# A sliding-window copy on one core: one row of the last plain unit leaves outside its scatter, in sixteen pieces

## The chip, the core and the metric

The kernel runs on one core of a Trainium2 chip. A core has several engines that work side by side, each with an instruction stream of its own: TensorE (PE, idle here), VectorE (DVE), ScalarE (ACT), GpSimd (POOL) and SyncE (SP). They work on SBUF, an on-chip memory of 128 partitions. Sixteen DMA engines move data between SBUF and device memory. A DMA is issued by SyncE, ScalarE or GpSimd, and is cut into packets that the DMA engines work off; when a DMA engine has done its share, it writes a 4-byte completion packet.

The metric is the time of one execution on the device in microseconds (us), as the median of several runs.

## The reference

The input x is a float32 tensor of 16 images with 64 channels of 64 x 64. Every 8 x 8 window at a stride of 4 is copied out, 15 x 15 windows for each image, with all channels. Nothing is computed; the kernel is data movement, 16.8 MB in and 62.9 MB out, since each input value lands in up to four windows.

```python
def reference(x, window_size, stride):          # 8 and 4
    n_h = n_w = 15
    result = np.zeros((batch, n_h, n_w, c, window_size, window_size), dtype=np.float32)
    for i in range(n_h):
        for j in range(n_w):
            h_start = i * stride
            w_start = j * stride
            result[:, i, j] = x[:, :, h_start:h_start + window_size, w_start:w_start + window_size].copy()
    return result
```

One output row, for an image and a window (i, j), is 64 channels x 8 x 8 floats: 4,096 floats, 16 KB in one piece of device memory.

## The kernel before

**Layout.** The input lies in the tile L. A partition is 64 * ch + 4 * b + q: ch is the half of the channels (2), b the image (16), q the quarter of the image's 64 rows (4). So partitions 0 to 63 hold the lower half of the channels and 64 to 127 the upper one. Of each quarter's 16 rows, a window may start at 4 slots, s = 0 to 3.

**Loads.** Part of the input comes first into the tiles of the output buffer GG, by DMAs of SyncE and ScalarE (L115), and is copied from there to L (L132). The rest is loaded straight into L by SyncE and GpSimd (L58).

**Units of work.** GG has four buffers of 16 KB for each partition; `tile_()` hands them out in turn. A unit fills one buffer so that each partition holds one finished output row, and then sends it out. Filling is copying with a column offset, by ScalarE (L164, L178, L203), by VectorE (copies, and stream shuffles at L167 and L174).

- `part(y, j)` (six times, L144 with idx_y0 or idx_y1) does the early work, on the half of the images that has been loaded first.
- `unit(j, 0)` is a plain unit: for window column j it fills slot 0 for partitions 0 to 63 and slot 1 for 64 to 127, and scatters with the index tile idx. It is done eight times, for j from 6 to 13.
- `unit(j, 2)` is a crossing unit for the slots 2 and 3, whose last windows reach into the next quarter. It scatters with idx_hi or idx_lo in turn, eight times with idx_lo and seven with idx_hi. In these a partition with q = 3 has no slot 3, and its row is skipped: its index is set beyond the bound that the scatter tests. In idx_lo these are the partitions 3, 7, ... 63, in idx_hi 67, 71, ... 127.
- At the end, window column 14 is done for slots 0 and 1 in two buffers (L251) and leaves by two plain stores of SyncE (L253), 64 rows of 16 KB each.

**Scatter.** `scatter` (L143) is one indirect DMA on GpSimd's queue: partition p's 16 KB go to the output row that the index tile names for p, plus a constant offset for j and s. An index of at least 16 * 225 is dropped. The stores are declared independent of each other (`free`), since each writes rows of its own.

**Order.** The program order is the order of the loops at L227 to L238: three parts; three pairs of a part and a plain unit; then five rounds of three crossing units and one plain unit. In the last round the plain unit (j = 13) has its copies split in another way between ScalarE and VectorE (the argument list with `ACT_C`), because the last plain unit is the last scatter; the two stores of SyncE come after it. The index tiles are computed once, at the start, by some twenty small integer operations of VectorE on 128 x 1 tiles (L72 to L101).

Of the kernel before, what the change touches and what calls it, by code (L numbers as in the profile page):

```python
# [10 lines left out]
def kernel(  # L11
# [7 lines left out]
    nc = tc.nc  # L19
# [10 lines left out]
    ALU = mybir.AluOpType  # L30
    CH = 2
    HQ = P // (B * CH)
    CL = C // CH
    RB = H // HQ
    NSLOT = RB // ST
# [26 lines left out]
    def itile(name):  # L62
        return ipool.tile([P, 1], i32, name=name)

    pi, tb, tq, tc_, th, idx, idx_y0, idx_y1, idx_lo, idx_hi = (
        itile(n) for n in ("pi", "tb", "tq", "tc", "th", "idx", "idx_y0", "idx_y1", "idx_lo", "idx_hi")
    )
    FAR = float(2 * B * NWIN)
    nc.gpsimd.iota(pi[:, :], pattern=[[0, 1]], base=0, channel_multiplier=1)  # L69

    def bits(d, shift, mask):
# [2 lines left out]
    def mul(d, a, m):  # L74
        nc.vector.tensor_scalar(out=d[:, :], in0=a[:, :], scalar1=float(m), scalar2=None, op0=ALU.mult)  # L75

    def tt(d, a, b, op):
        nc.vector.tensor_tensor(out=d[:, :], in0=a[:, :], in1=b[:, :], op=op)  # L78
# [14 lines left out]

    nc.vector.tensor_scalar(out=tq[:, :], in0=tq[:, :], scalar1=float(HQ - 1), scalar2=FAR, op0=ALU.is_equal, op1=ALU.mult)
    tt(th, tc_, tq, ALU.mult)
# [3 lines left out]
    tt(idx_lo, tb, th, ALU.add)  # L99
    mul(th, tc_, NW)  # L100
    tt(idx_lo, idx_lo, th, ALU.add)  # L101


    NG = 4
# [7 lines left out]
    for q in range(HQ):  # L112
        for ch in range(CH):
            s = S[ch][QP + q : QP + q + (B - 1) * HQ + 1 : HQ]
# [24 lines left out]
    def free(st):  # L139
        tc.declare_no_dep(st.ins, group="stores", reason="each store writes rows of its own")  # L140
        tc.add_to_no_dep_group("stores", st.ins)

    def scatter(g, ix, j, s):  # L143
        st = nc.gpsimd.indirect_dma_start(  # L144
            out=o_v,
            out_offset=bass.IndirectOffsetOnAxis(ap=ix[:, 0:1], axis=0),
            in_=g.rearrange("p c r w -> p (c r w)"),
            in_offset=None,
            element_offset=(s * NW + j) * CFREE,
            bounds_check=B * NWIN - 1,  # L150
            oob_is_err=False,
        )
        free(st)

    def fill(g, half, s, j, lo, n, copies):

        d = slice(half * HP + lo, half * HP + lo + n)
        cols = slice(j * ST, j * ST + WS)
        for ch in (half, 1 - half):
            f = slice(ch * HP + lo, ch * HP + lo + n)  # L160
            cs = slice(ch * CL, (ch + 1) * CL)
            copy = copies[ch != half]
            if s < NSLOT - 1:
                copy(out=g[d, cs, :, :], in_=L[f, :, s * ST : s * ST + WS, cols])  # L164
            else:
                copy(out=g[d, cs, 0:ST, :], in_=L[f, :, s * ST : RB, cols])
                nc.vector.stream_shuffle(out=g[d, cs, ST:WS, :], in_=L[f, :, 0:ST, cols], mask=nxt)  # L167

    act, dve = nc.scalar.copy, nc.vector.tensor_copy
# [6 lines left out]
    def split(k, other):  # L176
        def both(out, in_):
            act(out=out[:, 0:k], in_=in_[:, 0:k])  # L178
            other(out=out[:, k:], in_=in_[:, k:])  # L179

        return both

    mix = split(CL // 4, shf)
# [3 lines left out]
    ACT_C = 12  # L187
    at = 0

    def tile_():  # L190
        nonlocal at
        at += 1
        return G[(at - 1) % NG]
# [15 lines left out]

    crossed = 0  # L210

    def unit(j, s, copies=(shf, mix)):
        nonlocal crossed
        g = tile_()
        if s == 0:
            fill(g, 0, 0, j, 0, HP, (act, copies[0]))
            fill(g, 1, 1, j, 0, HP, (act, copies[1]))
            scatter(g, idx, j, s)
        else:

            turn = 1 - crossed % 2
            crossed += 1
            fill(g, turn, s, j, 0, HP, (act, act))
            fill(g, 1 - turn, s + 1, j, 0, HP, (shf, mix))
            scatter(g, (idx_hi, idx_lo)[turn], j, s)
# [3 lines left out]
    plain = [(j, 0) for j in range(2 * EARLY, NW - 1)]  # L229
    cross = [(j, 2) for j in range(NW)]  # L230
    for n in range(EARLY):
        part(1, 2 * n)
        unit(*plain.pop(0), (dve, dve))
    while plain:
        for w in cross[:3]:
            unit(*w)
        cross = cross[3:]
        unit(*plain.pop(0), *([] if len(plain) else [(split(ACT_C, shf), split(ACT_C, dve))]))  # L238


    o_e = out.rearrange("b i j c r w -> j b i (c r w)")
    j = NW - 1
    for s in range(2):
        g = tile_()
# [44 lines left out]
```

## Time and profile before

| what | value |
|---|---|
| median of 3 runs | 186.99 us (186.84 to 187.19) |
| profiled execution, time | 187.06 us |
| profiled execution, span from first to last instruction | 185.3 us |
| VectorE busy | 154.2 us, 83% |
| ScalarE busy | 150.7 us, 81% |
| GpSimd busy | 48.3 us, 26% |
| DMA packets | 10,980, 75.81 MB, mean 409 GB/s |
| GpSimd's DMA queue (q0) | 8,656 packets, 65.55 MB, 84.8% of the 16 engines' span |
| SyncE's DMA queue (q1) | 1,744 packets, 8.13 MB, 11.0% |
| ScalarE's DMA queue (q10) | 576 packets, 2.10 MB, 3.1% |
| instruction queue (q14) | 4 packets, 0.03 MB |

In a line on a group or on the timeline, "L144 POOL DMA_INDIRECT out_dram<-GG,idx" is the instruction at line 144, on GpSimd, that writes the output from GG with the index tile idx. "SPq" and "POOLq" are the instruction queues of SyncE and GpSimd; a time there is the time of issuing. A line with 40 digits cuts the span (or the window asked for) into 40 slices, and each digit is the busy share in tenths. In an answer on the DMA queues over a window, packets are counted by their start, and "under 512 B" counts the completion packets and other small ones. The trace also holds every DMA packet with its start, its time, its size and its queue, but not the number of its DMA engine; where a text speaks of packet records, it means these.

### The profile page before, as it was taken

How to read it: one execution, taken by the hardware profiler on the slowest of the kernel's cores; microseconds unless marked ns; L12 is line 12 of the kernel's file. 1: busy time of each engine (PE TensorE's matmuls, PEld its weight loads, DVE VectorE, ACT ScalarE, POOL GpSimd, SP SyncE). 2: the span in 40 equal slices, each digit the busy share in tenths (PEclk: the TensorE clock that was granted, in tenths of full speed). 3: DMA queues.
4: the chain of work that ended last, by engine and by line, in shares of the span. 5: the costliest groups of instructions: out<-in, count | busy, mean ns of one | idle time of the engine just before them, and what ended most of it. 6: DMA issues, size and time to landing. Idle time of an engine off the chain costs nothing.

```text
span 185.3 us, 597 instructions
## 1 busy us (share of the span) xinstructions
DVE 154.2 (83%) x213; ACT 150.7 (81%) x100; POOL 48.3 (26%) x50
## 2 busy tenths in 40 slices
DVE  5002998999999999799999999999999999999600
ACT  0002999999999999998899999998999999899600
POOL 7400652033308071422222222222222222222000
DMA  4999999999999999999999999999999999999995
GB/s 151 398 410 399 402 402 399 390 382 426 433 424 435 428 428 439 432 430 424 435 430 432 428 432 428 439 417 435 424 423 428 410 435 414 421 428 403 442 414 216
DMA packets 10980, 75.81 MB, mean 409 GB/s; under 512 B 3280, under 2 KB 3280, under 8 KB 7376
## 3 DMA queue, kind: packets, MB, share of 16 engines
q0 software_dynamic: 8656, 65.55, 84.8%
q1 hardware_dynamic: 1744, 8.13, 11.0%
q10 hardware_dynamic: 576, 2.10, 3.1%
q14 instruction: 4, 0.03, 0.0%
HBM read 16.78 MB, written 62.91 MB: 430 GB/s over the span
## 4 chain that ended last, share of the span: by engine, by line
ACT 28%; DVE 28%; DMA 27%; issue 8%; POOL 2%; ACTq 1%; DVEq 0%; PEldq 0%
DVE GG L174 17%; ACT GG L203 17%; DMA L<-in_x_dram 14%; DMA out_dram<-GG,idx 13%; DVE GG L167 11%; ACT GG L164 7%; ACT GG L251 3%; POOL L L58 2%; ACT GG L178 1%; ACTq L284 0%; ACTq L203 0%; POOL pi L69 0%; DVEq L174 0%; PEldq L284 0%; ACTq L164 0%
## 5 line engine op out<-in xcount | busy, mean ns | idle before, releaser
L164 ACT COPY GG<-L 64x2048 f32<-64x2048 f32 x46 | 87.3, 1897 | 5.1 <-DMA out_dram<-GG,idx 2.7
L174 DVE STREAM_SHUFFLE GG<-L 64x1024 f32<-64x1024 f32 (+4 forms) x39 | 53.0, 1359 | 1.3
L167 DVE STREAM_SHUFFLE GG<-L 64x1024 f32<-64x1024 f32 x30 | 38.4, 1281 | 0.0
L203 DVE COPY GG<-L 32x2048 f32<-32x2048 f32 x30 | 36.6, 1219 | 1.8 <-DMA L<-in_x_dram 0.8
L203 ACT COPY GG<-L 32x2048 f32<-32x2048 f32 x18 | 34.1, 1897 | 0.7 <-DMA L<-in_x_dram 0.3
L132 DVE COPY L<-GG 32x2048 f32<-32x2048 f32 x10 | 11.9, 1234 | 13.7 <-DMA GG<-in_x_dram 13.6
L144 POOL DMA_INDIRECT out_dram<-GG,idx_y x6 | 11.0, 1838 | 26.3 <-DVE GG L203 13.2
L58 POOL DMA_DIRECT2D L<-in_x_dram x16 | 12.8, 809 | 19.0 <-DMA L<-in_x_dram 18.5
L144 POOL DMA_INDIRECT out_dram<-GG,idx_lo x8 | 7.7, 961 | 30.8 <-DVE GG L167 23.2
L132 ACT ACT_TABLE_LOAD x1 | 1.3, 1283 | 17.2 <-DMA GG<-in_x_dram 17.2
L144 POOL DMA_INDIRECT out_dram<-GG,idx x8 | 9.7, 1217 | 17.4 <-DVE GG L174 6.8
L144 POOL DMA_INDIRECT out_dram<-GG,idx_hi x7 | 6.7, 961 | 26.6 <-DVE GG L167 22.9
L132 ACT COPY L<-GG 32x2048 f32<-32x2048 f32 x6 | 11.2, 1894 | 0.1
L178 ACT COPY GG<-L 64x256 f32<-64x256 f32 (+2 forms) x21 | 10.2, 484 | 0.5
L164 DVE COPY GG<-L 64x2048 f32<-64x2048 f32 x6 | 7.3, 1222 | 0.2
L251 DVE COPY GG<-L 32x1280 f32<-32x1280 f32 x8 | 6.5, 818 | 0.4 <-DMA out_dram<-GG,idx_hi 0.3
L251 ACT COPY GG<-L 32x768 f32<-32x768 f32 x8 | 6.6, 829 | 0.1
L174 DVE LOAD_MASK_SELECT GG<-L x39 | 0.4, 9 | 1.4 <-ACT GG L164 1.0
L72 DVE TENSOR_SCALAR tb<-pi 128x1 int32<-128x1 int32 x1 | 0.2, 154 | 1.0 <-POOL pi L69 1.0
L179 DVE COPY GG<-L 64x1280 f32<-64x1280 f32 x1 | 0.9, 877 | 0.0
L78 DVE TENSOR_TENSOR th<-tc,tq 128x1 int32<-128x1 int32 x2 | 0.3, 156 | 0.0
L75 DVE TENSOR_SCALAR th<-tc 128x1 int32<-128x1 int32 x2 | 0.3, 154 | 0.0
(21 smaller groups left out, 3.0 us busy)
## 6 DMA issues: line engine op xcount, KB each, us to landing
L<-in_x_dram POOLq DMA_DIRECT2D x10, 768.0 KB, 18.4
L<-in_x_dram SPq DMA_DIRECT2D x6, 640.0 KB
GG<-in_x_dram ACTq DMA_DIRECT2D x4, 512.0 KB, 14.4
GG<-in_x_dram SPq DMA_DIRECT2D x4, 512.0 KB, 14.8
out_dram<-GG SPq DMA_DIRECT2D x2, 1024.0 KB, 10.1
L<-in_x_dram POOLq DMA_DIRECT2D x6, 128.0 KB, 18.2
out_dram<-GG,idx POOLq DMA_INDIRECT x8, 12.4
out_dram<-GG,idx_lo POOLq DMA_INDIRECT x8, 10.3
```

The costliest lines, as they stand in the source:

```text
L58: eng.dma_start(out=L[p0 : p0 + QP - HQ + 1 : HQ, c0:c1, :, :], in_=x_v[ch, y, q, :, c0:c1, :])
L75: nc.vector.tensor_scalar(out=d[:, :], in0=a[:, :], scalar1=float(m), scalar2=None, op0=ALU.mult)
L78: nc.vector.tensor_tensor(out=d[:, :], in0=a[:, :], in1=b[:, :], op=op)
L132: tc.keep_in_program_order(copy(out=L[d, c : c + PC, :, :], in_=S[ch][f, c : c + PC]))
L144: st = nc.gpsimd.indirect_dma_start(out=o_v, out_offset=bass.IndirectOffsetOnAxis(ap=ix[:, 0:1], axis=0), in_=g.rearrange("p c r w -> p (c ...
L164: copy(out=g[d, cs, :, :], in_=L[f, :, s * ST : s * ST + WS, cols])
L167: nc.vector.stream_shuffle(out=g[d, cs, ST:WS, :], in_=L[f, :, 0:ST, cols], mask=nxt)
L174: nc.vector.stream_shuffle(out=out, in_=in_, mask=same)
L178: act(out=out[:, 0:k], in_=in_[:, 0:k])
L179: other(out=out[:, k:], in_=in_[:, k:])
L203: (act if n % 3 == 0 else dve)(out=g[d * QP : (d + 1) * QP, ch * CL : (ch + 1) * CL, :, :], in_=L[f : f + QP, :, s * ST : s * ST + WS, cols],)
L251: copy(out=g[d, ch * CL + c0 : ch * CL + c1, :, :], in_=L[f, c0:c1, s * ST : s * ST + WS, cols])
```

## The change

A further index tile, idx_one, is computed: it is idx, but for partition 12 the index is beyond the bound. In the last plain unit alone the scatter takes idx_one, so that it skips partition 12's row. This row, for image 3, quarter 0, slot 0 and window column 13, is sent by a direct DMA on GpSimd's queue, issued right behind the scatter. On both sides it is viewed as 16 pieces of 256 floats, 1 KB each.

```diff
+    ONE = 12
...
+    nc.vector.tensor_scalar(out=th[:, :], in0=pi[:, :], scalar1=float(ONE), scalar2=FAR, op0=ALU.is_equal, op1=ALU.mult)
+    tt(idx_one, idx, th, ALU.add)
...
-    def unit(j, s, copies=(shf, mix)):
+    def unit(j, s, copies=(shf, mix), one=False):
...
-            scatter(g, idx, j, s)
+            scatter(g, idx_one if one else idx, j, s)
+            if one:
+                row = out[ONE // HQ, ONE % HQ * NSLOT, j].rearrange("c r w -> (c r w)")
+                free(
+                    nc.gpsimd.dma_start(
+                        out=row.rearrange("(k n) -> k n", k=16),
+                        in_=g[ONE : ONE + 1].rearrange("p c r w -> p (c r w)").rearrange("p (k n) -> p k n", k=16),
+                    )
+                )
...
-        unit(*plain.pop(0), *([] if len(plain) else [(split(ACT_C, shf), split(ACT_C, dve))]))
+        unit(*plain.pop(0), *([] if len(plain) else [(split(ACT_C, shf), split(ACT_C, dve)), True]))
```

More of the change, by code (lines that the diff above doesn't have):

```diff
@@ L63, in itile @@
         return ipool.tile([P, 1], i32, name=name)
-    pi, tb, tq, tc_, th, idx, idx_y0, idx_y1, idx_lo, idx_hi = (
-        itile(n) for n in ("pi", "tb", "tq", "tc", "th", "idx", "idx_y0", "idx_y1", "idx_lo", "idx_hi")
+    pi, tb, tq, tc_, th, idx, idx_y0, idx_y1, idx_lo, idx_hi, idx_one = (
+        itile(n) for n in ("pi", "tb", "tq", "tc", "th", "idx", "idx_y0", "idx_y1", "idx_lo", "idx_hi", "idx_one")
     )
     FAR = float(2 * B * NWIN)
+    ONE = 12
     nc.gpsimd.iota(pi[:, :], pattern=[[0, 1]], base=0, channel_multiplier=1)
```

## The prediction

> **What bounds the kernel now.** I read the page from the top, then the busy time by stretch, the end of the timeline, SyncE's waits, and last the DMA queues in windows of a few tenths of a microsecond. First the span, the DMA line and the bytes:
>
> ```profile
> span 185.3 us, 597 instructions
> ...
> DMA  4999999999999999999999999999999999999995
> ...
> HBM read 16.78 MB, written 62.91 MB: 430 GB/s over the span
> ```
>
> The 16 DMA engines are full from the second of the 40 slices to the last. The stretches say the same, and that the compute engines stop about 10 us before the end:
>
> ```profile
> 50.00:95.00 45.00, 42.64 (x49) 42.70 (x26) 14.62 (x10) 1.00 1.01 430
> 95.00:170.00 75.00, 73.84 (x115) 71.44 (x53) 16.41 (x17) 1.00 1.01 426
> 170.00:175.00 5.00, 3.94 (x5) 4.31 (x6) 0.00 (x0) 1.00 1.00 419
> 175.00:180.00 5.00, 0.00 (x0) 0.00 (x0) 0.00 (x0) 1.00 1.00 426
> ```
>
> Columns: microseconds, busy VectorE, ScalarE and GpSimd, clock, DMA share, GB/s. So DMA work sets the end, and the question is which engine of the 16 ends last. The last issues, and SyncE's last waits:
>
> ```profile
> 168.09 1.03 POOL L144 DMA_INDIRECT out_dram<-GG,idx  x1 [1.42 <-ACT GG L178]
> ...
> 171.03 3.97 SPq L253 DMA_DIRECT2D out_dram<-GG  x2
> ```
>
> ```profile
> SPq L284 <- DMA out_dram<-GG,idx: 7.4, 1, 7.4
> ...
> SPq L284 <- DMA out_dram<-GG: 1.5, 1, 1.5
> ```
>
> The scatter that the change edits is the last one; two stores of SyncE follow, and the program waits for these last. Every DMA ends on each engine with a 4-byte packet, so the queues in two neighbouring windows, 182.9 to 183.4 and 183.4 to 184.1 us, show who is late:
>
> ```profile
> DMA packets 15, 0.00 MB, mean 0 GB/s; under 512 B 15, under 2 KB 15, under 8 KB 15
> ...
> DMA packets 2, 0.02 MB, mean 23 GB/s; under 512 B 1, under 2 KB 1, under 8 KB 1
> ```
>
> Fifteen engines post their last completion by 183.38; one then starts a whole 16 KB row, alone, and ends at 184.03 (packet records). **One engine is a row behind, and it alone is the end.** It is so for the last scatter too: 15 completions from 180.54 to 180.92, the sixteenth at 182.18.
>
> Which engine is it? In each scatter with idx_lo the rows of partitions 3, 7, ... 63 are skipped, and a skipped row leaves a 4-byte packet. Eight engines then show two groups of three rows and such a packet: each serves two groups of four neighbouring partitions of 0 to 63. The late one is among them (windows 171.5 to 171.72 and 172.2 to 172.5 us, first skipped packets of the last such scatter):
>
> ```profile
> DMA packets 17, 0.16 MB, mean 745 GB/s; under 512 B 7, under 2 KB 7, under 8 KB 7
> ...
> DMA packets 7, 0.10 MB, mean 328 GB/s; under 512 B 1, under 2 KB 1, under 8 KB 1
> ```
>
> And why is it late? Joined end to start (a packet begins 3 to 4 ns before the one ahead of it on its engine ends), the records give it two of the four 8 KB instruction packets, at 50.58 and 134.76 us:
>
> ```profile
> q14 instruction: 1, 0.01, 3.9%
> ...
> q14 instruction: 1, 0.01, 4.8%
> ```
>
> Each took 0.309 us, and the row behind it 1.020 and 0.956 instead of 0.611: 1.36 us in all. VectorE had 65 recorded instructions before the first and 193 before the second, 128 apart, so these are VectorE's. The other two, at 80.54 and 95.35, sit on two other engines of the same eight.
>
> **The change part by part.** *Two index operations on VectorE*: 0.154 + 0.16 us by their neighbours' rows, in the 13.6 us in which VectorE waits for the loads. Nothing; without that cover 0.3 us. VectorE's 262 recorded instructions become 264, GpSimd's 126 some 129; the next 8 KB packets would come after 321 and about 190, so none is added.
>
> *The skipped row.* Eight rows and a completion take 4.862 us on an undisturbed engine, 0.607 a row. Partition 12's engine loses 0.607 and gains a 4-byte packet, 0.006: −0.601 us there and nothing elsewhere.
>
> *The pieces.* One more issue on GpSimd right behind the scatter, from about 169.1 us. Its direct issues take 0.55 to 0.81 us, nothing is queued behind it there, and SyncE's stores wait for copies alone. The scatter's rows keep the engines' queues busy until 180.5, so it has 10 us of cover; without that it costs under a microsecond on GpSimd, and still nothing at the end. No tile is taken again after it.
>
> A piece of 1 KB is in no row. Through 4 KB (0.155 us from start to start) and 16 KB (0.607) runs 0.0377 us per KB, which gives 0.042 us; below that it cannot be. The other end is the dearest thing a small packet did here: the 0.41 us by which the row behind an instruction packet was stretched, so 0.45 with the piece. I take 0.042: the pieces ride in the scatter's own queue, where 4-byte packets leave the next row at 0.611. With 0.006 for the completion, each engine gains 0.048.
>
> *Sum.* If partition 12 is on the late engine: −0.601 + 0.048 = −0.553 us, end at 183.48. The next engine ends at 183.38 + 0.05 = 183.43, so the gain is 0.553 and could at most be 0.605. The profiled execution, 185.28 of span and 1.78 around it, is 187.06, 0.07 above the median; it would become 186.51, the median 186.44, 0.30% less. I say 186.45.
>
> Is it that engine? No view numbers them. By count among eight it is 1 in 8, and the other end is certainty. [...] I judge 0.75, nearer to the upper end. [...]
>
> **The rivals.** *A, the partition takes it back.* All pieces come from partition 12. The late engine reads its rows at 16,384 B in 0.607 us, 27.0 GB/s. If that is the pace of its partitions' way out and not of the engine, the 15 pieces that other engines fetch take 15 × 0.0377 = 0.565 us from it: −0.553 + 0.565 = +0.01, 187.0. For it: rows keep that pace to a few ns for 40 us together. Against: nowhere do two engines visibly share partitions, so no slowing of that kind is seen. [...]
>
> *B, another engine.* Partition 12 lies on an engine that ends 0.65 us or more earlier. Then the late one keeps its rows and gets its piece: +0.048, 187.04.
>
> *C, slower.* One mechanism: the piece stretches the late engine's next row as the instruction packets did, 0.45 us, and that engine has kept its row: +0.46, 187.45. It decides from a piece of 0.37 us on. For it: two stretched rows on this very engine. Against: the other two instruction packets stretched theirs by 0.11 and 0.08 only, and the late engine comes to its piece at 182.2, when the others have fetched theirs.
>
> *D, one packet instead of sixteen.* If the row leaves in one 16 KB packet on one engine, that one ends at 183.63 to 183.99 in place of 184.03: 186.6 to 186.95.
>
> **How the numbers follow.** The forecast, late engine relieved and pieces cheap, 0.48: 186.45. A 0.22, B 0.10, C 0.17, D 0.03. What a measurement of this kernel can tell from no change is about 0.2%, 0.37 us. Faster is the forecast and most of D, 0.50; same is A, B and the rest of D, 0.33; slower is C, 0.17. The forecast's own range is 186.3 to 186.65, from the 0.605 cap and the spread of 186.84 to 187.19. The one for 8 in 10 runs from 186.25 over A and B to 187.3, and leaves out most of C.
>
> **What would show it.** A right forecast shows 16 completions within half a microsecond at the end, SyncE's two last waits together 8.3 us instead of 8.9, 16 packets of 1 KB around 180.6 to 181.6, and no lone row. A shows no row more on the late engine, but rows stretched while the pieces pass. B shows the lone row and one engine ending early. C shows the lone row and a long one behind a piece. It goes wrong first where the link from VectorE's instruction packets to partition 12 fails, then where one partition cannot feed sixteen engines beside its own.

## The result

The change made the kernel slower: 187.79 us (187.62 to 187.96) against 187.08 us for the kernel before, measured beside it; the ratio is 1.0041, with a 95% interval of 1.0029 to 1.0052. The forecast was 186.45 us, with a range of 186.3 to 186.65. The profiled execution's span went from 185.28 to 186.19 us, 0.905 us more. That is more than the medians differ by, 0.71, since the profiled execution of the changed kernel is the slowest of its six (187.96 us).

The page of the changed kernel shows the same full queues, and the sixteen pieces of 1 KB as the difference between the counts under 2 KB and under 512 B (3,313 − 3,297):

```profile
span 186.2 us, 600 instructions
...
DMA  4999999999999999999999999999999999999994
...
DMA packets 11012, 75.81 MB, mean 407 GB/s; under 512 B 3297, under 2 KB 3313, under 8 KB 7409
```

**The late engine was relieved.** These are the two queues of the changed kernel in the window from 180.7 to 181.2 us (packets, MB, share):

```profile
q1 hardware_dynamic: 32, 0.26, 135.8%
q0 software_dynamic: 16, 0.00, 1.8%
```

All sixteen completions of the last scatter (q0) stand together, from 180.79 to 181.17 us. In the kernel before, fifteen stood together and the sixteenth came 1.27 us behind them. So partition 12 does lie on the engine that was a row behind.

**And yet it ends last again.** The completions of the closing stores, in the windows from 183.3 to 184.0 and from 184.0 to 184.4 us:

```profile
DMA packets 17, 0.03 MB, mean 47 GB/s; under 512 B 15, under 2 KB 15, under 8 KB 15
...
DMA packets 1, 0.00 MB, mean 0 GB/s; under 512 B 1, under 2 KB 1, under 8 KB 1
```

Fifteen are there by 183.95, one at 184.33. The packet records of this one engine, from the scatter's completion on, say where the relief went:

```text
start us   took us   bytes   queue
181.094    0.009         4   q0    the last scatter's completion
181.113    1.324    16,384   q1    a row of the closing store: 0.611 elsewhere
182.433    0.047     1,024   q0    its piece
182.479    0.632    16,384   q1
183.107    0.009         4   q0    the pieces' completion
183.113    0.611    16,384   q1
183.720    0.615    16,384   q1
184.334    0.007         4   q1    the store's completion
```

While the other fifteen engines fetched their pieces from partition 12, this engine read a row of its own, and this one row took 1.324 us, 0.713 more than a row takes. The pieces on the others took from 0.046 to 0.255 us.

**The program no longer ends with the stores.** The closing instructions of GpSimd and SyncE, before (first fence) and after (second); a line gives the shortest, median and longest time in ns, then the first and the last start in us:

```profile
L284 POOLq EVENT_SEMAPHORE  x4: 17/17/17, 184.5 to 185.2; - x4
L284 POOLq DRAIN  x3: 51/105/16551, 167.9 to 185.0; - x3
L284 SPq DRAIN  x3: 7/7/7, 184.4 to 184.8; - x3
```

```profile
L295 POOLq EVENT_SEMAPHORE  x4: 17/17/17, 185.4 to 186.1; - x4
L295 POOLq DRAIN  x3: 46/111/16946, 168.4 to 185.9; - x3
L295 SPq DRAIN  x3: 7/7/13, 184.7 to 185.7; - x3
```

These drains stand at the end of an engine's program; on GpSimd the first one is recorded from 0.22 us (before) and 0.75 us (after) ahead of its last issue on, and lasts until 167.87 + 16.55 = 184.42 us before, and until 168.45 + 16.95 = 185.40 after. GpSimd's closing semaphore steps follow at 184.5 and 185.4. SyncE had its part done at 184.51 before, a little later than GpSimd; after the change it is done at 184.82 and waits. It shows in SyncE's waits, too, before (first fence) and after (second); the columns are the wait in all, how often, and the longest. The view names PE's queue, but in both kernels SyncE goes on 0.04 us after GpSimd's second semaphore step, at 184.66 and 185.56 us:

```profile
SPq L284 <- PEq L284: 0.7, 2, 0.5
```

```profile
SPq L295 <- DMA out_dram<-GG: 9.1, 2, 8.3
...
SPq L295 <- PEq L295: 1.3, 2, 0.8
```

So two paths were close to each other at the end, 0.09 us apart, and the change lengthened both: the stores' path by 0.31 us, the drain's by 0.98. The drain ends 2.23 us after the last completion in GpSimd's queue before (182.18), and 2.29 us after it in the changed kernel (183.11).

### The profile page after: what moved, and what is told of

Read it like the earlier page. It is cut to its first block, busy times and chain, and to the rows that moved or that the text cites. A ratio compares the mean times of both kernels' runs of the same rounds, so it can differ in the third digit from the quotient of the medians.

```text
span 186.2 us, 600 instructions
## 1 busy us (share of the span) xinstructions
DVE 154.5 (83%) x215; ACT 150.7 (81%) x100; POOL 50.0 (27%) x51
## 2 busy tenths in 40 slices
DMA packets 11012, 75.81 MB, mean 407 GB/s; under 512 B 3297, under 2 KB 3313, under 8 KB 7409
## 4 chain that ended last, share of the span: by engine, by line
DMA 34%; ACT 28%; DVE 24%; issue 6%; ACTq 1%; SPq 0%; DVEq 0%
ACT GG L206 17%; DVE GG L177 14%; DMA out_dram<-GG,idx 13%; DMA L<-in_x_dram 11%; DVE GG L170 9%; ACT GG L167 7%; DMA out_dram<-GG,idx_hi 6%; DMA GG<-in_x_dram 4%; ACT GG L262 3%; ACT GG L181 1%; DVE GG L206 1%; ACTq L295 0%; SPq L58 0%; ACTq L118 0%; ACTq L206 0%
## 5 line engine op out<-in xcount | busy, mean ns | idle before, releaser
L58 POOL DMA_DIRECT2D L<-in_x_dram x16 | 13.7, 863 | 18.2 <-DMA L<-in_x_dram 17.6
L147 POOL DMA_INDIRECT out_dram<-GG,idx x7 | 8.7, 1240 | 16.0 <-DVE GG L177 6.8
L147 POOL DMA_INDIRECT out_dram<-GG,idx_one x1 | 1.0, 1037 | 1.4 <-ACT GG L181 1.4
L225 POOL DMA_DIRECT2D out_dram<-GG x1 | 0.8, 804 | 0.0
```

The source lines that it names most:

```text
L58: eng.dma_start(out=L[p0 : p0 + QP - HQ + 1 : HQ, c0:c1, :, :], in_=x_v[ch, y, q, :, c0:c1, :])
L147: st = nc.gpsimd.indirect_dma_start(out=o_v, out_offset=bass.IndirectOffsetOnAxis(ap=ix[:, 0:1], axis=0), in_=g.rearrange("p c r w -> p (c ...
L225: nc.gpsimd.dma_start(out=row.rearrange("(k n) -> k n", k=16), in_=g[ONE : ONE + 1].rearrange("p c r w -> p (c r w)").rearrange("p (k n) - ...
```

## The experiments

The theory after this reading has two causes. First, partition 12 can be read only at the pace of one engine, so that the pieces take back from the late engine (0.71 us) what the skipped row had given (0.60). Second, GpSimd's closing drain ends some 2.25 us after the last completion in GpSimd's queue, and the pieces make this completion late. The times of before are those measured beside each kernel.

**The row left out.** This is the relief by itself.

```diff
             scatter(g, idx_one if one else idx, j, s)
-            if one:
-                ...
```

> Partition 12's row is skipped in the last plain unit and not sent at all; one output row is left out. Theory: the late engine is relieved, its last completions of the scatter and of the stores come 0.60 us earlier, both ends follow, 0.55 to 0.60 us below before: some 186.5. Rival (partition 12 is not on the late engine): no change within 0.1 us, and a lone row at the end as before.

Measured: 186.41 us against 187.02, ratio 0.9973 (0.9963 to 0.9983). No row is left alone at the end; in the window from 182.8 to 183.36 us all sixteen completions are there:

```profile
DMA packets 16, 0.00 MB, mean 0 GB/s; under 512 B 16, under 2 KB 16, under 8 KB 16
```

The relief of 0.6 us is real, and the prediction's choice of the engine was right. What follows has to explain 1.3 us between this, 0.61 us below before, and the changed kernel, 0.71 above.

**The pieces' stretch without the relief.** The scatter keeps partition 12 and skips 108.

```diff
-    ... scalar1=float(ONE), scalar2=FAR, op0=ALU.is_equal, op1=ALU.mult)
+    ... scalar1=float(ONE + 96), scalar2=FAR, op0=ALU.is_equal, op1=ALU.mult)
...
-                row = out[ONE // HQ, ONE % HQ * NSLOT, j]...
+                row = out[(ONE + 32) // HQ, ONE % HQ * NSLOT + 1, j]...
```

> The scatter skips partition 108 and keeps 12; the sixteen pieces are still read from 12, and go to the row that 108 would have sent, which so holds other data. The late engine gets the pieces' stretch without any relief. Theory: its stores end 0.75 us later than before, its last completion in GpSimd's queue comes at about 183.7, the drain at 185.9: 1.3 to 1.5 us above before, some 188.5. Rival (no stretch by the partition, the drain alone): the last completion in GpSimd's queue at 182.8 to 183.1, the drain at 185.1 to 185.4, 0.6 to 0.9 us above before.

Measured: 188.97 us against 187.02, ratio 1.0106 (1.0091 to 1.0121). The sign and the order are the theory's, the size is beyond it. One row of the late engine took 1.289 us, its stores ended at 184.71 us, 0.68 later than before, and the last completion in GpSimd's queue came at 184.09, not at 183.7: the stretched row was the late engine's last scatter row, the scatter's completion came at 182.82, and then the piece and its completion each came behind a store row. The drain ended at 186.37, 2.28 us behind that completion.

**The pieces from another partition.**

```diff
-                        in_=g[ONE : ONE + 1]...
+                        in_=g[ONE + 96 : ONE + 97]...
```

> The pieces are read from partition 108 instead of 12, still on GpSimd's queue; partition 12 is still skipped, so that one output row gets the data of another. Theory: the 0.71 us stretch goes to the engine that serves partition 108; the relieved engine keeps all its rows at 0.61 us and posts its last completion of the stores some 0.7 us earlier than in the changed kernel. GpSimd's last completion still comes late, at 182.4 to 183.0, so that the drain still ends at 184.6 to 185.3 and the time lies 0.1 to 0.75 us above before. Rival (the stretch comes from the pieces as such and not from their partition): the same engine is stretched as in the changed kernel, 0.7 us above before.

Measured: 187.80 us against 187.02, ratio 1.0044 (1.0032 to 1.0056). The late engine's rows now take 0.61 to 0.63 us from 174 us on, and it ends by 183.7. Another engine has one row of 1.273 us, from 180.89 on, and this one ends last, at 184.07. It has no skipped rows in the scatter with idx_lo ahead, so it serves partitions of the upper half, as 108 is. So the stretch goes with the partition, as the theory has it. The last completion in GpSimd's queue, at 182.84, belongs to this engine as well, and the drain ends at 185.12: alone it keeps the time where it was.

**The pieces ahead of the scatter.**

```diff
+            if one:
+                ...                      # the sixteen pieces, as they were
             scatter(g, idx_one if one else idx, j, s)
-            if one:
-                ...
```

> The pieces are issued on GpSimd's queue ahead of the last scatter instead of behind it; partition 12 as in the changed kernel. Theory: the stretched row of the relieved engine stays (0.6 to 0.7 us, so its end stays 0.1 to 0.3 us behind that of the kernel before), but the last completion in GpSimd's queue is the scatter's again, at 182.2 to 182.4, and the drain ends at 184.4 to 184.7 instead of 185.4: 0.1 to 0.3 us above before. Rival (the extra DMA on GpSimd costs what it costs wherever it is issued): 0.7 us above before, as in the changed kernel.

Measured: 187.15 us against 186.99, ratio 1.0009 (1.0000 to 1.0017). This takes away the second cause alone. A row of 1.213 us is still there, at 172.7, and the stores end at 183.90 (184.03 before), so 0.13 us is left of the relief of 0.60. But the last completion in GpSimd's queue is the scatter's, at 181.92, and the drain ends at 184.19, ahead of SyncE's part (184.38). Of the 0.71 us that the changed kernel lost, 0.16 is left. So most of what the extra DMA cost lay in its place in the queue.

**The last store on GpSimd's queue.** This is the drain alone: the kernel before, with nothing skipped and no pieces.

```diff
-        free(nc.sync.dma_start(out=o_e[j, ...
+        free((nc.sync, nc.gpsimd)[s].dma_start(out=o_e[j, ...
```

> The kernel before with one change: the second of the two closing stores goes out on GpSimd's queue instead of SyncE's. The bytes and their engines are the same. Theory (GpSimd's closing drain ends 2.2 to 2.4 us after the last completion in its queue): the last completion there comes at about 184.0, the drain ends at 186.3, 1.6 to 1.9 us above before. Rival (the drain waits for nothing but its own issues, or overlaps the landing): within 0.3 us of before.

Measured: 188.71 us against 186.99, ratio 1.0093 (1.0080 to 1.0106). The data end at 183.82 us, no later than before, and the drain ends at 186.09, 2.27 us behind. SyncE's waits of this kernel:

```profile
SPq L284 <- DMA out_dram<-GG: 12.7, 1, 12.7
SPq L284 <- PEq L284: 2.1, 2, 1.6
```

The second line is the wait for GpSimd, 1.6 us where it was 0.5. In all fourteen profiled kernels of this study the first drain ended between 2.23 and 2.42 us after the last completion in GpSimd's queue.

**The pieces on SyncE's queue.**

```diff
-                    nc.gpsimd.dma_start(
+                    nc.sync.dma_start(
```

> The pieces leave on SyncE's queue instead of GpSimd's, nothing else is changed. Theory (two causes: reading partition 12 from sixteen engines stretches one 16 KB row of the relieved engine by 0.71 us, so that the relief of 0.60 is taken back; and GpSimd's closing drain ends 2.25 us after the last completion in GpSimd's queue, which the pieces push from 182.18 to 183.11 us): the drain no longer counts, the stretched row stays, 0.1 to 0.3 us above the kernel before, some 187.2 to 187.4 where before is 187.08. Rival 1 (the stretched row alone is the whole loss, the drain is only a spectator): 0.7 us above before, as in the changed kernel. Rival 2 (the extra DMA on GpSimd is the whole loss, the relief is real): 0.55 us below before.

Measured: 188.16 us against 187.02, ratio 1.0060 (1.0047 to 1.0073), and none of the three had foreseen it. The edit did not do what its text says. This is the count of this kernel's packets, and its issue:

```profile
DMA packets 10983, 75.81 MB, mean 406 GB/s; under 512 B 3283, under 2 KB 3283, under 8 KB 7379
...
out_dram<-GG SPq DMA_DIRECT2D x1, 16.0 KB
```

There is no packet between 512 B and 2 KB: from SyncE the same view of 16 by 256 left as one packet of 16 KB on one engine. The instruction's own record already has one element of 16,384 bytes, where GpSimd's has sixteen of 1,024, so the pieces were joined before the instruction ran. That is a cleaner look at the first cause than the one that was planned. At 170.7 us this packet took 1.375 us, and a row that another engine began at 170.9 took 1.131, the only two of that length. That is about what two packets of 16 KB need if they share one way out, 2 × 0.607 = 1.21 us. The engine that got the extra packet ended at 184.88, and its last completion in GpSimd's queue came at 183.66, so that the drain ended at 185.90: both causes again.

**Neither cause on the late engine.** The pieces ahead of the scatter and from partition 108, and then from partition 28.

```diff
-                        in_=g[ONE : ONE + 1]...      # in the kernel with the pieces first
+                        in_=g[ONE + 96 : ONE + 97]...  # 108; then ONE + 16 : ONE + 17, 28
```

> The pieces are issued ahead of the last scatter and read from partition 108, so that one output row gets the data of another. Neither of the two causes is left on the late engine. Theory: that engine's rows all take 0.61 to 0.63 us and it ends 0.55 us earlier; the engine of partition 108 has the stretched row instead and ends at 183.7 to 184.1; last completion in GpSimd's queue by 181.7. 0 to 0.4 us below before, and at least 0.2 us below the same order with partition 12. Rival (order alone matters, the partition does not): the same time as with partition 12.

> The pieces ahead of the last scatter, read from partition 28 instead of 108 (one output row gets the data of another). Partition 28 lies in the half whose engines end later. Theory: the late engine keeps unstretched rows and ends 0.55 us earlier; the engine of partition 28 takes the stretched row and ends 0.1 us above to 0.4 below the old end: 186.6 to 187.2. If the time is again 187.4 or more, with the two causes absent, something else in this order costs time, and that stays open.

Measured: 187.57 us for 108 (186.94 to 188.09), against 186.99, ratio 1.0032 (1.0019 to 1.0045); 187.16 us for 28, against 186.98, ratio 1.0013 (1.0004 to 1.0022). With 28 it went as expected: the engine that had the row of 1.229 us ended last, at 184.16, and the second by 183.84. Moving the source chose which engine pays, and this one paid what the late engine had gained. Whether an engine with more room would do better isn't shown: in the kernel before the other fifteen ended between 183.01 and 183.37 us, 0.65 to 1.0 ahead of the late one. With 108 the expectation failed. Its runs spread over 1.15 us, where those of the other kernels spread over 0.2 to 0.7, and the profiled one, 187.15, is among the lowest. In it the late engine was relieved and the stretched one ended at 183.37, but a third one ended last, at 184.09. Why this kernel spreads was not settled.

**The row from another partition and by its own engine.** The block of partitions 0 to 31 is copied once more, to partitions 96 to 127 of a buffer that is half free, and a scatter of its own sends partition 108's row, ahead of the last scatter.

```diff
+        if one:
+            spare = G[at % NG]
+            for ch, copy in ((0, shf), (1, act)):
+                copy(out=spare[3 * QP : P, ch * CL : (ch + 1) * CL, :, :],
+                     in_=L[ch * HP : ch * HP + QP, :, 0:WS, j * ST : j * ST + WS])
+            scatter(spare, idx_far, j, s)
```

> Partition 12's row is skipped in the last scatter; ahead of it the block of partitions 0 to 31 is copied once more, into partitions 96 to 127 of the buffer that the first closing store uses at 32 to 95, and a scatter of its own sends partition 108's row from there. So the row leaves by another partition and by the engine that serves it, ahead of the last scatter. Theory: the late engine is relieved by 0.60, all engines gain 0.05 by the skipped rows' small packets, the engine of partition 108 gains 0.61 and ends at 183.6 to 184.0 in place of the late one's 184.03; the drain ends at 183.9 to 184.1 and no longer counts: 0 to 0.35 us below before. Rival (the two more copies, 1.3 us on VectorE and 1.9 us on ScalarE, let the queues run dry before the closing stores): 0.5 us or more above before.

Measured: 187.05 us against 186.99, ratio 0.9998 (0.9990 to 1.0007). No row is stretched, and the drain ends at 182.60 and does not count. But the added copies and the added scatter put the issue of the last scatter from 168.09 to 172.12 us, and the queues ran dry:

```profile
165.00:170.00 5.00, 4.32 (x4) 3.92 (x3) 0.96 (x1) 1.00 1.01 429
170.00:175.00 5.00, 4.46 (x6) 4.51 (x6) 3.02 (x2) 1.00 0.64 269
175.00:180.00 5.00, 2.09 (x3) 2.13 (x3) 0.00 (x0) 1.00 0.98 419
```

From 170 to 175 us the DMA engines are busy 64% of the time, 1.8 us lost on each. That the time is still that of before came in part from elsewhere: from 130 to 170 us its rows took 0.612 us on average, where those of the kernels told of so far took 0.622 to 0.624. It has two index tiles more than the kernel before, which moves the output buffers. So this was tried alone.

**The output buffers moved.** Unused small tiles ahead of them: one, as many as the change adds; two, as in the kernel just told of; and six.

```diff
+    for n in range(1):          # 2, 6
+        nc.vector.memset(itile(f"pad{n}")[:, :], 0)
```

> The kernel before with one more small index tile, set to zero and never used, so that the output buffers start where they do in the changed kernel. Theory (the pieces are the whole loss): within 0.15 us of before. Rival (moving the output buffers by one tile costs time by itself, and part of the changed kernel's loss is that): 0.2 to 0.7 us above before.

> The kernel before with two more unused tiles, so that the output buffers start where they do in the kernel that sends the row from elsewhere, whose rows took 0.611 us from 120 to 170 us where those of all other kernels took 0.622. Rival (the place of the buffers sets that): rows of 0.611 us there, and 0.4 to 0.8 us below before. Theory (it comes from how the engines' rows stand to each other in time, not from the place): rows of 0.62 us, within 0.15 us of before.

> The kernel before with six unused tiles. One more tile changed nothing (187.03), two more gave 186.11 and rows of 0.611 us to the end. If the output buffers have to start at a multiple of four tiles (12 tiles in all with two more, 16 with six), the rows stay at 0.611 us here too and the time is 186.0 to 186.4. If any shift by more than one tile does it, the same, so only a miss tells these apart. If the gain belongs to the one place that two tiles give, the rows go back to 0.622 us from 130 us on and the time is 186.9 to 187.2.

Measured: 187.03 us with one against 186.98, ratio 1.0000 (0.9991 to 1.0009); 186.11 us with two, ratio 0.9952 (0.9938 to 0.9965); 187.15 us with six against 186.91, ratio 1.0012 (1.0003 to 1.0021). The same stretches with two tiles and with six:

```profile
130.00:150.00 20.00, 19.66 (x31) 18.78 (x14) 3.85 (x4) 1.00 1.01 431
150.00:170.00 20.00, 19.71 (x32) 19.14 (x17) 4.89 (x5) 1.00 0.99 424
```

```profile
130.00:150.00 20.00, 19.66 (x31) 18.83 (x14) 3.85 (x4) 1.00 1.01 424
150.00:170.00 20.00, 19.71 (x31) 19.04 (x16) 4.88 (x5) 1.00 1.00 420
```

With one tile the time stays, so the change's own extra tile is not a part of its loss. With two, the mean row from 135 to 165 us is 0.612 us (0.623 before), and the kernel beats both that this study began with. That six do not help rules out that any shift by more than one, or any multiple of four tiles in all, does it. The unused tiles also add instructions of VectorE that set them to zero; the kernel that sends the row from elsewhere has no such instructions, as many tiles and the same short rows, which speaks for the place of the buffers and does not prove it.

## Why the prediction was wrong

- **The bound and the late engine** were right: the DMA engines set the end, one of them was a row behind, and partition 12 lies on it. The kernel without the row shows it, −0.61 us where the relief was put at −0.60. That the packets at 50.58 and 134.76 us are VectorE's is borne out too: in the kernel with six unused tiles, which has six more VectorE instructions at the start, they come at 35.57 and 130.53 us, while the other two stay (80.11 and 95.48). But that this engine "alone is the end" was wrong, as told below. The step from VectorE's packets to partition 12, put at 0.75, was my estimate: no view of the kernel before shows it; the changed kernel's completions and the kernel without the row do.
- **The two index operations and the tile** cost nothing, as said (1.0000 with one more tile).
- **"I take 0.042" as all that the pieces cost** is the first step that failed. The late engine's own piece did take 0.047 us. But the other fifteen took the row beside it from 0.611 to 1.324 us: a term of 0.71 that the forecast's sum left out. It is rival A, which put it at 0.565 and had a chance of 0.22; in six kernels the stretched row was 0.60 to 0.71 us above a plain one, wherever the pieces were read, and in a seventh two whole packets side by side took 1.375 and 1.131 us. On the stores' path the sum is −0.60 + 0.05 + 0.71 = +0.16 us. The profiled execution shows +0.31; the late engine was already 0.13 us behind its time of before at 174 us, with none of the change yet in its queue. By rival A the forecast would have been 187.0, nearer, and still too low.
- **"Still nothing at the end"** for the issue on GpSimd is the second, and on the profiled executions it cost more. I counted what waits behind the DMA on GpSimd and found nothing; but the program's end waits for GpSimd's drain, 2.2 to 2.4 us after the last completion in its queue. In the kernel before, that path ended 0.09 us ahead of the stores' path, and the prediction's profile lines didn't look at it. A piece that rides behind the scatter, in turn with the rows of the stores, put that completion from 182.18 to 183.11 us: the scatter's last completion came 1.09 us earlier, then came the stretched row and the piece (1.39 us), a store row (0.63) and the completion. The pieces themselves ran from 181.44 to 182.48 us, where the prediction had 180.6 to 181.6; it had left out the store rows between.
- **Without the first cause there was still no gain to be had in this form.** This is an estimate from the rows above, and no run shows it: with an unstretched row the pieces' completion would come at 181.09 + 0.62 + 0.05 + 0.61 = 182.37, no earlier than before, and the drain would end at 184.6. Both steps had to hold for 186.45.
- **Of the rivals**, C had the sign and about the size (187.45 against 187.79), with another mechanism: it gave the stretch to an engine that had kept its row, and had no drain in it, so that it came near by luck. B is excluded by the sixteen completions, D by the sixteen packets.

## What to carry to other kernels

Before work is moved off the engine that ends last, list every path that the program's end waits for, each queue's drain too, with the time by which it is early; a path that was 0.09 us early here became the bound. A row cut into sixteen pieces for many engines still stretched one engine's row in six kernels here, by 0.60 to 0.71 us on 0.61, and this engine, which reads the partition for its own rows, paid for all the pieces. And what was put at the end of GpSimd's queue moved that queue's last completion by 0.93 us, from 182.18 to 183.11, though the row taken off had brought the scatter's own forward by 1.09.

## What the runs showed that was not expected

GpSimd's closing drain ended 2.23 to 2.42 us after the last completion in its queue in each of the profiled kernels; with the last store of the program on GpSimd's queue instead of SyncE's, and nothing else changed, the time was 188.71 us against 186.99, 1.7 us more.

The same view of a row, 16 by 256 floats, left as sixteen packets of 1 KB on GpSimd's queue and as one of 16 KB on SyncE's; the issuing instructions already differ in it.

An 8 KB instruction packet stretched the row behind it on its engine by 0.08 to 0.41 us in the kernel before.

Two unused index tiles made the kernel 0.48% faster (186.11 us), with rows that stay at 0.612 us on average; one tile and six did not. What in the place of the buffers, or in the times that it sets, does it is open; it wasn't traced further.
